# Expert stage of a two-layer decoder trunk: from 128-slot blocks per expert with weights cut in two to 32-slot units packed into five blocks with weights in plain float32

## The chip, the cores and the metric

The kernel runs on one core of a Trainium2 chip. The metric is device time in microseconds of one execution. Times are medians over the runs shown; everything read from a profile belongs to one profiled execution, whose span is given with it.

## The reference

256 tokens of width 1024 pass through two layers. Each layer has a mixer part (an S5 scan, retention and stick-breaking attention side by side), a norm, a feed-forward part and a second norm. Layer 0 has a dense SwiGLU; layer 1, the subject here, has a router with 8 experts of hidden width 688, of which each token takes the best two.

```python
def moe_swiglu(x, w_router, e_gate, e_up, e_down):
    xt = x.reshape(-1, d)                               # 256 x 1024
    logits = (xt @ w_router).astype(F32)                # 256 x 8
    top_val, top_idx = lax.top_k(logits, TOP_K)         # TOP_K = 2
    top_w = jax.nn.softmax(top_val, axis=-1)
    gates = jnp.sum(jax.nn.one_hot(top_idx, N_EXPERTS) * top_w[..., None], axis=1)
    out = jnp.zeros(xt.shape, F32)
    for e in range(N_EXPERTS):
        out = out + gates[:, e:e + 1] * swiglu(xt, e_gate[e], e_up[e], e_down[e])
    return out

def swiglu(x, w_gate, w_up, w_down):                    # 1024x688, 1024x688, 688x1024
    return (jax.nn.silu(x @ w_gate) * (x @ w_up)) @ w_down
```

Everything is float32. Of the 512 pairs of token and expert, the reference's routing of these inputs gives the eight experts 50, 75, 58, 31, 91, 61, 47 and 99.

## The kernel before

**Layout of the work.** Tokens stand in two tiles of 128 (t = 0, 1). All large products of the kernel are made of float32 numbers cut into two float32r parts: `mm3` makes three passes, high by high, high by low and low by high, into one PSUM bank. [...]

**The weight stream.** `Stream` holds one list of weight pieces in the order of use. A piece is up to 128 x 1032 numbers (516 KB). SyncE issues its DMA into a tile `st` (`load`, L361), ScalarE copies it as float32r to `wh` (L376), and VectorE, or GpSimd for some pieces, subtracts that from `st` to make `wl` (L380). Six `st` tiles, five pairs `wh`/`wl`, and four further `st2` tiles in the expert stage bound how far the stream runs ahead. The stream goes through both layers without a break, so the first pieces of the experts are loaded and cut while the mixers of layer 1 still run. `done` of a piece issues the load of a later one.

**The expert stage before.** `route` makes the logits of a token tile and the 0/1 choice `sel`; `places` ranks the tokens of each expert by a triangular matmul, and `one_hots` (L1202) makes from the ranks, per expert, a 128 x 128 matrix `Pf` (token by slot). Each expert has 128 slots. `gather(pr)` multiplies the tokens' two parts by the `Pf` of two experts: `xe_h`, `xe_l` hold 2 x 128 slots by 1024 (L1275, L1277). `gu` makes gate and up of one expert and one half of its hidden columns: 8 k tiles, each `mm3` of 128 slots by 344 columns. `prep` transposes and cuts the hidden values, `down` makes 6 k tiles by 1024 columns, and `y_h`, `y_l` (L1371, L1372) are the weighted results in two parts, which `scatter` sends back to the tokens with the transposed one-hots `PT`. A second pass over all weights follows if some expert has more than 128 tokens; here none has. The tail is the last norm and the DMAs of the output (L1474).

**What sets the order.** Each engine runs its instructions in one fixed order, worked out when the program is built, mostly that of the code. PSUM has eight banks (`Bank()`), given out in turn. Tiles of a pool with `bufs=n` rotate, and a new pool's tiles may lie where a closed pool's tiles lay; their first writer then waits for the last readers of those. The pool `mix` holds what the mixers need and is closed before the expert stage, whose pool `moe` takes its place.

Of the kernel before, what the change touches and what calls it, by code (L numbers as in the profile page):

```python
# [26 lines left out]
DFE = 688  # L27
DFP = 704
HFE = 344
NE = 8  # L30
TWO_PI = 2.0 * math.pi
# [8 lines left out]
for _n, _w in (("ident", 128), ("ntri", 128), ("nones", 128), ("blk64", 128), ("blk16", 128),  # L40
               ("rank", 128), ("iota", 128), ("i32", 32), ("sel", 8),
               ("iota8", 8)):
    CST[_n] = (_o, _o + _w)
    _o += _w
NCST = _o


def host_constants():
# [12 lines left out]
    put("iota", np.broadcast_to(p[None, :], (128, 128)))  # L61
    put("i32", (p[:, None] % 32 == np.arange(32)[None, :]))
    put("sel", (p[:, None] % 32 == np.arange(8)[None, :]))
    put("iota8", np.broadcast_to(np.arange(8)[None, :], (128, 8)))
    half = 32
# [25 lines left out]
KSPLIT = {256: (4, 4), 2 * FL: (2, 2, 2, 2), HFE: (3, 3, 2)}  # L91
KFIRST = (2, 2, 4)
HALVES = ((0, 512), (512, D))
CUTS = ((0, 512), (512, 768), (768, D))


def tiles_of(w, c0, n, split=None):
    """the column block [c0, c0 + n) of w [1024, .] as consecutive [128, kt * n] pieces"""
    out, k0 = [], 0
    for kt in split or KSPLIT[n]:  # L100
        out.append(w[k0 * 128:(k0 + kt) * 128, c0:c0 + n].reshape(kt, 128, n).transpose(1, 0, 2).reshape(-1))
        k0 += kt
    return out


def layout(inp):
    """the operands in the order in which the kernel reads them; nothing but moves and zero padding"""
# [32 lines left out]
    for n in ("moe_w_gate", "moe_w_up"):  # L140
        w[n] = np.concatenate([p for x in a[n] for y in x for hf in range(2) for p in tiles_of(y, hf * HFE, HFE)])
# [4 lines left out]
    w["moe_w_down"] = np.pad(a["moe_w_down"].reshape(-1, D), ((0, DFP - DFE), (0, 0)))  # L146
# [8 lines left out]
class Lanes:  # L155
# [15 lines left out]
    def urgent(self, gen, all_steps):  # L171
        """the first step, or all steps, issued ahead of what was emitted before them"""
# [26 lines left out]
PM = 2  # L199
# [5 lines left out]
URG2 = 60  # L205
# [7 lines left out]
def trunk(ctx, tc, I, out, dbg=None, layers=2):  # L213
# [5 lines left out]
    wst = ctx.enter_context(tc.tile_pool(name="wst", bufs=NST))  # L219
    whl = ctx.enter_context(tc.tile_pool(name="whl", bufs=NHL))  # L220
    act = ctx.enter_context(tc.tile_pool(name="act", bufs=1))
    psum = ctx.enter_context(tc.tile_pool(name="psum", bufs=8, space=PSUM))

# [3 lines left out]
    # functions that live in different tables keep their order of emission, so that tables change seldom  # L227
# [3 lines left out]
    def behind(x, y):  # L231
        """x after y in the order of their engine"""
# [18 lines left out]
    class Bank:  # L251
# [21 lines left out]
    def mm_narrow(b, o, h, wh, wl):  # L273
        """h: 64 rows of high parts over their low parts; wh: the high parts of 64 weight rows, twice"""
# [15 lines left out]
    # ---------------------------------------------------------------- weight stream  # L290
# [3 lines left out]
    def add_cols(key, name, n, specs=specs, split=None):  # L294
        """next column block of the array `name`"""
# [12 lines left out]
    def plan_moe(specs):  # L308
        def gu(e, hf):
            for part, name in (("g", "moe_w_gate"), ("up", "moe_w_up")):  # L310
                pos_in[name] = (2 * e + hf) * D * HFE
                add_cols((part, e, hf), name, HFE, specs)

        def dn(e):
            for k in range(6):
                add_rows(("dn", e, k), I["moe_w_down"], e * DFE + k * 128, min(128, DFP - k * 128), specs)

        for e in range(0, NE, 2):
            gu(e, 0)
            gu(e, 1)  # L320
            gu(e + 1, 0)
            dn(e)
            gu(e + 1, 1)
            dn(e + 1)

    for l in range(layers):
# [12 lines left out]
        else:  # L339
            plan_moe(specs)  # L340

    class Stream:
        def __init__(self, specs):
            self.specs = specs
            self.ld = self.sp = self.used = 0
            self.extra, self.ahead = None, NST
            self.act_after = self.dve_after = None
# [3 lines left out]
        def load(self):  # L351
# [4 lines left out]
            if self.extra is not None and i % 10 >= 6:  # L356
                st = self.extra.tile([128, CW], F32, name="st2", bufs=4)
            else:
                st = wst.tile([128, CW], F32, name="st")
# [5 lines left out]
        def split(self):  # L365
# [10 lines left out]
            x = S.activation(hv, st, AF.Copy)  # L376
            if self.act_after is not None:
                behind(x, self.act_after)
            on_pool = (self.extra is not None and i % 5 == PM) or i in self.pool_lo
# [3 lines left out]
            elif self.dve_after is not None:  # L383
                behind(x, self.dve_after)
# [17 lines left out]
        def done(self, key):  # L402
# [4 lines left out]
            while self.sp < self.used + NHL and self.sp < len(self.specs):  # L407
# [3 lines left out]
               + [((1, "u"), 0)] + [(("g", 0, 0), k) for k in range(2)])  # L411
# [17 lines left out]
    def ln_stats(sm, away=False, part=None):  # L429
        """mean (12), rstd (15), -mean * rstd (16)"""  # L430
# [12 lines left out]
    def ln_apply(t, r, y, sm, w_bc, b_bc, h, away=False):  # L443
        c = slice(h * 512, (h + 1) * 512)
        if away:
            # on the engines beside the vector engine
            W.act_after = S.activation(y[:, c], r, AF.Identity, scale=sm[:, 15:16], bias=sm[:, 16:17])
# [22 lines left out]
    # ---------------------------------------------------------------- S5 operands of a layer  # L470
    def s5_pre(l, mp, q, E):
        """what depends on the layer's parameters alone; q: the queue that loads them, E: the engine of the larger products"""
# [59 lines left out]
        # e^{4 i theta}  # L532
# [12 lines left out]
        def after(x):  # L545
            """behind the weights' splits that the engine has to make by now"""
# [6 lines left out]
        # rotation tables cos, sin of 4 theta c and the decay r^4 (0 where a pair's row begins)  # L553
# [20 lines left out]
        # input operands a^{3-i} Bbar, block-diagonal over the two groups of a pair  # L574
# [12 lines left out]
        # output operands C a^{j+1}: re, -im  # L587
# [21 lines left out]
        # within-chunk operator  # L609
# [43 lines left out]
    def rms_rstd(pool, b, cols, sq, blk, tag, bufs=2):  # L653
        """mean of squares over channel blocks by a block matrix; returns rstd tile [128, n]"""
# [7 lines left out]
    # ---------------------------------------------------------------- one layer's mixers  # L662
# [155 lines left out]
    late = []  # L818
    LNL = {}

    def layer(l, mp):
# [135 lines left out]
            # output projection: rows of the finished parts first  # L957
# [21 lines left out]
            for t in range(2):  # L979
# [16 lines left out]
            if l % 2:  # L996
                late.extend((l, "o", k) for k in order[5:])
                L.drain()
            for k in order[4:5] if l % 2 else order[4:]:
                W.done((l, "o", k))  # L1000
            W.act_after = None
            W.dve_after = RT.get("hot")
# [5 lines left out]
    # ---------------------------------------------------------------- dense SwiGLU  # L1008
    def ffn(l, fp):
# [20 lines left out]
            # the last, narrow block first and with the tokens stationary: it starts on the first token tile alone  # L1030
# [69 lines left out]
    # ---------------------------------------------------------------- top-2 of 8 experts  # L1100
# [412 lines left out]
```

## Time and profile before

| | us |
|---|---|
| median of 3 runs (743.38 to 743.99) | 743.42 |
| span of the profiled execution | 744.1 |
| PE busy in the span | 693.4 (93%) |
| VectorE, ScalarE, GpSimd busy | 552.8, 454.9, 266.4 |
| bytes read from HBM | 146.42 MB |

PE is TensorE's matmuls, PEld its weight loads, DVE VectorE, ACT ScalarE, POOL GpSimd and SP SyncE, whose busy time is not counted; a "q" behind an engine's name is its sequencer. The busy share over the whole span mixes the mixers of two layers, a dense feed-forward part, the router at about 475 to 500 us and the expert stage from there to the end. The change touches the program from the router on, so the windows from 490 us to the end are what is to be read.

### The profile page before, as it was taken

How to read it: one execution, taken by the hardware profiler on the slowest of the kernel's cores; microseconds unless marked ns; L12 is line 12 of the kernel's file. 1: busy time of each engine (PE TensorE's matmuls, PEld its weight loads, DVE VectorE, ACT ScalarE, POOL GpSimd, SP SyncE). 2: the span in 40 equal slices, each digit the busy share in tenths (PEclk: the TensorE clock that was granted, in tenths of full speed). 3: DMA queues.
4: the chain of work that ended last, by engine and by line, in shares of the span. 5: the costliest groups of instructions: out<-in, count | busy, mean ns of one | idle time of the engine just before them, and what ended most of it. 6: DMA issues, size and time to landing. Idle time of an engine off the chain costs nothing. (4 is left out here: it accounts for less than half of the span.)

```text
span 744.1 us, 12592 instructions
## 1 busy us (share of the span) xinstructions
PE 693.4 (93%) x4812; PEld 621.4 (84%) x4812; DVE 552.8 (74%) x756; ACT 454.9 (61%) x665; POOL 266.4 (36%) x245
## 2 busy tenths in 40 slices
PE   6989899989999999999899999968999999999993
PEld 6988777778999999988798887758889889899882
DVE  5998957588655455558867476599999986889976
ACT  5646686455444444453447985347878884888862
POOL 1734611599970000005014220354534322323441
PEclk9979999989999999999999999969999999999997
DMA  8844453356566666662473262338989987988911
GB/s 326 294 148 168 117 182 100 106 165 223 165 198 190 184 192 186 186 194 88 146 220 116 85 200 77 103 122 285 362 283 331 343 285 269 297 301 296 346 34 61
DMA packets 43987, 148.36 MB, mean 199 GB/s; under 512 B 5328, under 2 KB 5456, under 8 KB 43920
## 3 DMA queue, kind: packets, MB, share of 16 engines
q1 hardware_dynamic: 43776, 147.23, 60.5%
q8 instruction: 39, 0.64, 0.4%
q14 instruction: 28, 0.23, 0.1%
q10 hardware_dynamic: 144, 0.26, 0.1%
HBM read 146.42 MB, written 1.05 MB: 198 GB/s over the span
## 5 line engine op out<-in xcount | busy, mean ns | idle before, releaser
L380 DVE TENSOR_TENSOR wl<-st,wh 128x1024 fp32r<-128x1024 f32 (+4 forms) x235 | 308.8, 1335 | 111.8 <-ACT wh L376 111.2
L376 ACT ACTIVATE wh<-st 128x1024 fp32r<-128x1024 f32 (+5 forms) x275 | 275.4, 1020 | 159.7 <-PE bank L257 135.8
L380 POOL TENSOR_TENSOR wl<-st,wh 128x1024 fp32r<-128x1024 f32 (+4 forms) x40 | 100.6, 2521 | 274.5 <-ACT wh L376 274.4
L257 PE MATMUL bank<-xth,wh 128*128 128x256 f32 x608 | 175.1, 288 | 0.0
L257 PE MATMUL bank<-xtl,wh 128*128 128x256 f32 x608 | 172.5, 284 | 0.0
L257 PE MATMUL bank<-xth,wl 128*128 128x256 f32 x608 | 172.3, 283 | 0.0
L257 PEld LDWEIGHTS bank<-xth,wh 128*128 128x128 f32 x608 | 116.2, 191 | 2.0 <-issue 0.9
L257 PEld LDWEIGHTS bank<-xth,wl 128*128 128x128 f32 x608 | 116.1, 191 | 0.8 <-issue 0.5
L257 PEld LDWEIGHTS bank<-xtl,wh 128*128 128x128 f32 x608 | 116.0, 191 | 0.8 <-issue 0.2
L257 PE MATMUL bank<-wl,xe_h 128*128 128x344 f32 x256 | 82.1, 321 | 2.5 <-DVE wl L380 2.5
L257 PE MATMUL bank<-wh,xe_h 128*128 128x344 f32 x256 | 83.3, 325 | 0.0
L257 PE MATMUL bank<-wh,xe_l 128*128 128x344 f32 x256 | 81.9, 320 | 0.7 <-DVE xe_l L1277 0.7
L257 PEld LDWEIGHTS bank<-wl,xe_h 128*128 128x128 f32 x256 | 48.3, 189 | 3.1 <-DVE wl L380 3.1
L257 PEld LDWEIGHTS bank<-wh,xe_h 128*128 128x128 f32 x256 | 48.4, 189 | 1.8 <-ACT wh L376 1.0
L257 PEld LDWEIGHTS bank<-wh,xe_l 128*128 128x128 f32 x256 | 48.1, 188 | 1.0 <-DVE xe_l L1277 0.9
L257 PE MATMUL bank<-wl,hT_h 128*128 128x512 f32 (+3 forms) x102 | 40.5, 397 | 0.0
L257 PE MATMUL bank<-wh,hT_h 128*128 128x512 f32 (+1 forms) x102 | 39.8, 390 | 0.0
L257 PE MATMUL bank<-wh,xth 128*128 128x256 f32 (+1 forms) x112 | 31.3, 320 | 7.5 <-ACT wh L376 6.4
L257 PE MATMUL bank<-wh,f_h 128*128 128x512 f32 x88 | 35.3, 401 | 0.1
L257 PE MATMUL bank<-wl,f_h 128*128 128x512 f32 (+1 forms) x88 | 35.0, 397 | 0.0
L257 PE MATMUL bank<-wh,f_l 128*128 128x512 f32 x84 | 33.2, 397 | 1.7 <-DVE f_l L419 1.7
L257 PE MATMUL bank<-wh,hT_l 128*128 128x512 f32 (+1 forms) x85 | 32.6, 383 | 0.0
(301 smaller groups left out, 1234.9 us busy)
## 6 DMA issues: line engine op xcount, KB each, us to landing
st<-in_w_in_dram SPq DMA_DIRECT2D x47, 512.0 KB, 4.1
st<-in_moe_w_down_dram SPq DMA_DIRECT2D x40, 512.0 KB, 5.6
st<-in_moe_w_gate_dram SPq DMA_DIRECT2D x32, 516.0 KB, 5.5
st<-in_moe_w_up_dram SPq DMA_DIRECT2D x32, 516.0 KB, 5.2
st<-in_ffn_w_down_dram SPq DMA_DIRECT2D x21, 512.0 KB, 4.3
st<-in_ffn_w_gate_dram SPq DMA_DIRECT2D x20, 512.0 KB, 4.3
st<-in_ffn_w_up_dram SPq DMA_DIRECT2D x20, 512.0 KB, 4.3
st<-in_w_out_dram SPq DMA_DIRECT2D x16, 512.0 KB, 3.9
```

The costliest lines, as they stand in the source:

```text
L257: PE.matmul(o, lhsT, rhs, start=part not in self.begun, stop=True, skip_group_check=True)
L376: x = S.activation(hv, st, AF.Copy)
L380: x = (G if on_pool else V).tensor_tensor(lv, st, hv.bitcast(F32), op=OP.subtract)
```

## The change

Tokens of an expert sit in **units** of 32 slots. Four units make a block of 128 slots, and there are five blocks, 20 units. Fifteen units belong to fixed experts (two to each of experts 0 to 6, one to expert 7: units 1 to 3 of block j belong to expert (3j + u - 1) // 2). The first unit of each block is free: an expert with more than 64 tokens (32 for expert 7) takes free units in turn, and which expert a free unit belongs to is computed on the chip by `places`, written to `unit` and loaded into a TensorE register for each block. If more than five free units are needed, the whole stage runs again on the tokens left over, and a third time above ten. By the counts above the experts need 0, 1, 0, 0, 1, 0, 0 and 3 free units.

A product of one k tile and one block is now four matmuls in plain float32 with 32 slots each, whose results go to partitions 0, 32, 64 and 96 of one bank; the first reads its weights at an address from the register. The loops are turned: k tile by k tile, and in it the five blocks with all experts. For this the weights lie in memory k tile by k tile for all eight experts: a **chunk** `ch` is 128 rows by 8 x 344 numbers, 1.409 MB, loaded by two DMAs of 704 KB, and a ring of 7 chunks runs ahead. There are 32 chunks for gate and up (2 hidden halves x 2 matrices x 8 k tiles) and 18 for down (3 cuts of the output columns x 6 k tiles of 128, 128 or 96 rows), 68.16 MB. No expert weight is cut in two any more. The stream of the earlier stages ends with layer 1's `w_out`, and its pools are closed ahead of the expert stage.

The main parts of the diff (what `Stream` no longer needs, `host_constants`, the removed `gu`, `prep`, `down` and `scatter`, and the second pass are left out):

```diff
+        w[n] = np.ascontiguousarray(a[n][0].reshape(NE, KT, 128, 2, HFE).transpose(3, 1, 2, 0, 4)).reshape(-1)
...
-                            normed(0, *zs[0], lnw[:, 0], lnw[:, 1])
-                            places(0)
-                            RT["hot"] = places(1)
-                            normed(1, *zs[1], lnw[:, 0], lnw[:, 1])
+                            places()
+                            for t_ in range(2):
+                                normed(t_, *zs[t_], lnw[:, 0], lnw[:, 1])
...
+    def places():
+        pb = Bank()
+        pb.mm(pb.t[:, 0:8], rank_b[:, 0], sel[:, 0])
...
+        V.tensor_tensor(over, pb.t[:, 16:24], C["cap"], op=OP.subtract)
+        V.tensor_copy(pos, pb.t[:, 0:16].rearrange("p (t e) -> p t e", t=2))
...
+        V.tensor_scalar(ui[:, 0:16], eu, float(NE - 1), None, op0=OP.min)
...
+    def one_hots(p, pool):
+        for t in range(2):
+            sl = RT["slots"][:, :, 0:wb]
+            V.tensor_scalar(tmp, sl, nm[:, t, 0:1], None, op0=OP.is_equal)
+            V.scalar_tensor_tensor(P[:, t], sl, nm[:, t, 1:2], tmp, op0=OP.is_equal, op1=OP.add)
...
+    class Chunks:
...
+            t = self.pool.tile([128, NE * HFE], F32, name="ch", bufs=NCH)
+            v = t[:rows, 0:NE * cols]
+            for h in range(2):
+                n = NE * cols // 2
+                SP.dma_start(v[:, h * n:(h + 1) * n], bass.AP(tensor=ap.tensor, offset=ap.offset + o + h * n, ap=[[NE * cols, rows], [1, n]]))
...
     def moe(l):
         with tc.tile_pool(name="moe", bufs=1) as mp:
-            W.extra, W.ahead = mp, 10
-            while W.ld < min(W.sp + W.ahead, len(W.specs)):
-                W.load()
+            with tc.high_priority(offset=URG):
+                RT["P"] = one_hots(0, mp)
+            first_chunks = Chunks(mp)
...
+                unit = [nc.values_load(RT["unit"][0:1, p * NDYN + j:p * NDYN + j + 1], engines=[mybir.EngineType.PE], min_val=0, max_val=NE - 1)
+                        for j in range(NB)]
...
+                    for k, o in ((0, Pg[:, t]), (1, Pw)):
+                        G.tensor_scalar(o, RT["slots"][:, :, 0:wb], nm[:, t, k:k + 1], gates[:, t, k:k + 1], op0=OP.is_equal, op1=OP.mult)
...
+                def units(b, o, lhs, j, ch, cols):
+                    b.mm(o[0:32], lhs[:, j * wb:j * wb + 32], ch[:, bass.ds(unit[j], 1), :].rearrange("p a n -> p (a n)"), part=0)
+                    if not p:
+                        for u in range(1, 4):
+                            b.mm(o[32 * u:32 * u + 32], lhs[:, j * wb + 32 * u:j * wb + 32 * u + 32], ch[:, (3 * j + u - 1) // 2, :], part=u)
+
+                def project(name, hf, between=()):
+                    acc = [Bank() for _ in range(NB)]
+                    for kt in range(KT):
+                        if kt in between:
+                            between[kt]()
+                        ch = WM.get(name, hf, kt)
+                        for j in range(NB):
+                            units(acc[j], acc[j].t[:, 0:HFE], xe[:, kt], j, ch, HFE)
+                        WM.done(name, hf, kt)
+                    return acc
...
+                def hidden(hf):
+                    gt = project("moe_w_gate", hf, {} if hf else {0: lambda: gather(range(4)), 4: lambda: gather(range(4, 8))})
+                    for j in range(NB):
+                        fn(ms[:wb, j], gt[j].t[:wb, 0:HFE], AF.Silu)
+                    up = project("moe_w_up", hf, {4: weigh} if not hf else {})
+                    for j in range(NB):
+                        V.tensor_tensor(hs[:wb, j, 0:HFE], ms[:wb, j], up[j].t[:wb, 0:HFE], op=OP.mult)
+                        for k in range(3):
+                            b.tr(b.t[:, k * wb:(k + 1) * wb], hs[:wb, j, k * 128:(k + 1) * 128], ident[:wb, :wb])
...
+                for c, (c0, c1) in enumerate(DCUTS):
+                    for k in range(6):
+                        ch = WM.get("down", c, k)
+                        for j in range(NB):
+                            units(acc[j], acc[j].t[:, 0:w], hT[:rows, k // 3, k % 3], j, ch, w)
+                        WM.done("down", c, k)
...
+            total = nc.values_load(RT["unit"][0:1, 16:17], min_val=0, max_val=16)
+            with tc.If(total > NDYN):
+                experts(1, Chunks(mp))
```

Two places show how instructions move. The first is SyncE's queue at the end of the weights of layer 1's `w_out` (`st` is a tile of the old stream, `ch` half a chunk of the new one). Before:

```order
L361 DMA st<-in_w_out_dram 128x1024 [waits DMAHW6_49,DVE_49]
L361 DMA st<-in_moe_w_gate_dram 128x1032 [waits DVE_49]
L361 DMA st<-in_moe_w_gate_dram 128x1032 [waits DMAHW0_49,DVE_49,Activation_49]
L361 DMA st<-in_moe_w_gate_dram 128x688 [waits DMAHW1_49,DVE_49]
L361 DMA st<-in_moe_w_up_dram 128x1032 [waits DMAHW4_49,DMAHW2_49,DVE_49]
```

And with the change:

```order
L361 DMA st<-in_w_out_dram 128x1024 [waits DVE_49]
L1274 DMA ch<-in_moe_w_gate_dram 128x1376 [waits DMAHW3_49,DMAHW2_49,DMAHW4_49,DMAHW0_49,DMAHW5_49,DVE_49,DMAHW6_49,PE_49,DMAHW7_49,Activation_49,Pool_49]
L1274 DMA ch<-in_moe_w_gate_dram 128x1376 [waits DMAHW1_49]
L1274 DMA ch<-in_moe_w_gate_dram 128x1376 x6
...
L1292 DMA lnw<-in_ln_ffn_w_dram 128x1024 [waits DMAHW6_49]
L1293 DMA lnw<-in_ln_ffn_b_dram 128x1024 [waits DMAHW7_49]
L1274 DMA ch<-in_moe_w_gate_dram 128x1376 [waits DMAHW0_49,PE_49]
```

The first expert weights waited only for a piece to be cut; now the first chunk waits for all engines, the next thirteen halves for nothing but queues, and from the fifteenth on for a chunk that TensorE has read.

The second place is TensorE at the end of the gather (`Pf` or `P` is the one-hot matrix, `xe` the gathered tokens, `wh`/`wl` parts of a cut weight). Before:

```order
L257 MATMUL bank<-Pf_5177,xl 128x256 x5
L257 MATMUL bank<-wh,xe_h 128x344 [waits DMAHW3_49,DMAHW4_49,DMAHW2_49,DMAHW5_49,DMAHW1_49,DMAHW6_49,DMAHW0_49,DMAHW7_49,Activation_49,Pool_49]
L257 MATMUL bank<-wl,xe_h 128x344
L257 MATMUL bank<-wh,xe_h 128x344 [waits Activation_49]
L257 MATMUL bank<-wl,xe_h 128x344 [waits DVE_49]
```

And with the change:

```order
L281 MATMUL bank<-P_5202,xl 128x128
L281 ISA
L281 MATMUL bank<-ch,xe 32x344 [waits DMAHW1_49,DMAHW0_49,Activation_49]
L281 MATMUL bank<-ch,xe 32x344 x3
L281 ISA
L281 MATMUL bank<-ch,xe 32x344 x4
L281 ISA
```

Three full matmuls per k tile and expert have become four of 32 partitions per k tile and block, each four behind a register operation (`ISA`) that forms the address of the free unit's weights.

## Rows read from the trace of the kernel before

**Rows 1.** Windows by stage: us; busy PE, PEld, DVE, ACT, POOL (count); PEclk; DMA share; GB/s.

```profile
490.00:512.00 22.00, 17.85 (x99) 16.86 (x100) 20.10 (x51) 13.41 (x21) 11.21 (x7) 0.73 0.64 214
512.00:700.00 188.00, 185.93 (x1081) 168.15 (x1080) 167.49 (x176) 148.69 (x191) 66.41 (x34) 1.00 0.91 311
...
712.00:731.00 19.00, 18.87 (x105) 15.68 (x103) 13.20 (x20) 8.21 (x13) 7.35 (x4) 1.00 0.00 0
731.00:744.10 13.10, 0.92 (x6) 0.71 (x6) 6.99 (x12) 2.85 (x7) 3.15 (x2) 0.62 0.24 87
```

**Rows 2.** The chain around the first expert work: start us, duration us, engine, line, operation.

```profile
489.48 1.27 POOL L448 TENSOR_TENSOR xtok<-xtok,lnw 128x512 f32<-128x512 f32 x1 [3.56 <-ACT xtok L447]
...
489.69 1.08 DVE L1160 SCALAR_TENSOR_TENSOR rtw<-rtw,ln_s,rneg 128x8 f32<-128x8 f32 x1
...
492.41 2.25 DVE L1163 CAST rtw<-ix 128x2 f32<-128x2 uint32 x1
...
495.44 0.22 DVE L1165 SCALAR_TENSOR_TENSOR sel<-cst,rtw 128x8 bf16<-128x8 f32 x1
...
501.28 0.49 PE L257 MATMUL bank<-wh,xe_h 128*128 128x344 f32 x1
```

**Rows 3.** SyncE's queue in the 50 us before the expert stage, same columns.

```profile
445.28 7.05 SPq L361 DMA_DIRECT2D st<-in_moe_w_gate_dram  x3
```

**Rows 4.** Windows with the DMA engines filled, columns as in the first group.

```profile
520.00:540.00 20.00, 20.00 (x110) 17.60 (x109) 19.70 (x19) 16.94 (x22) 11.32 (x5) 1.00 1.01 361
580.00:600.00 20.00, 20.00 (x111) 17.60 (x110) 16.35 (x17) 15.34 (x20) 7.94 (x3) 1.00 1.00 363
...
584.00:592.00 8.00, 8.00 (x35) 5.93 (x35) 7.78 (x6) 6.51 (x8) 2.75 (x2) 1.00 1.02 405
```

**Rows 5.** DMA queue of the weights, 488 to 712: packets, MB, share of 16 engines.

```profile
q1 hardware_dynamic: 19504, 65.87, 85.8%
```

**Rows 6.** Groups of instructions from 490 to 712: busy us, mean ns, idle before.

```profile
L257 PE MATMUL bank<-wh,xe_h 128*128 128x344 f32 x254 | 82.7, 325 | 0.0
...
L380 DVE TENSOR_TENSOR wl<-st,wh 128x1032 fp32r<-128x1032 f32 x50 | 70.0, 1429 | 6.2 <-ACT wh L376 6.2
...
L1331 DVE TENSOR_TENSOR hs<-m_s,bank 128x344 f32<-128x344 f32 x15 | 7.6, 506 | 4.9 <-PE bank L257 4.7
...
L249 ACT ACTIVATE m_s<-bank 128x344 f32<-128x344 f32 x16 | 7.1, 444 | 0.7 <-PE bank L257 0.7
```

**Rows 7.** TensorE in the router, float32 with 32 output columns: start us, duration us.

```profile
474.93 0.43 PE L257 MATMUL bank<-xt,rw 128*32 128x128 f32 x8
475.28 0.50 PE L257 MATMUL bank<-wh,mtl 128*128 128x512 f32 x1
```

**Rows 8.** The 32-wide router matmuls by themselves: duration ns min/median/max.

```profile
L257 PE MATMUL bank<-xt,rw x32: 272/285/297, 474.9 to 488.1; 128*32 128x128 f32 x32
```

**Rows 9.** TensorE in the scan's operands of layer 0, full-width matmuls: same columns.

```profile
101.23 0.28 PE L257 MATMUL bank<-xth,wl 128*128 128x256 f32 x1
101.35 1.89 PE L257 MATMUL bank<-s5g,prm 128*128 128x256 f32 x8
```

**Rows 10.** TensorE in the same scan, 64-wide float32 matmuls: same columns.

```profile
87.13 0.98 PE L257 MATMUL bank<-s5e,vmat 128*64 128x63 f32 x26
```

**Rows 11.** Register operations at the branch: duration ns min/median/max.

```profile
L1480 SPq FUSED_REGOPS  x1: 191/191/191, 706.6 to 706.6; - x1
...
L1480 PEldq TENSOR_LOAD <-cmi x1: 487/487/487, 731.4 to 731.4; - x1
```

**Rows 12.** A window with TensorE two thirds busy, columns as in the first group.

```profile
350.00:356.00 6.00, 4.00 (x38) 3.76 (x36) 6.00 (x4) 0.00 (x0) 5.16 (x2) 1.00 0.55 184
```

**Rows 13.** The last scatter, columns as in the second group.

```profile
730.37 0.47 ACT L1371 ACTIVATE y_h<-bank,gs 128x256 fp32r<-128x256 f32 x1 [2.50 <-PE bank L257]
730.88 0.48 DVE L1372 SCALAR_TENSOR_TENSOR y_l<-bank,gs,y_h 128x256 fp32r<-128x256 f32 x1 [0.40 <-ACT y_h L1371]
...
731.47 0.45 PE L257 MATMUL bank<-y_l,PT 128*128 128x256 f32 x2
```

More of the change, by code (lines that the diff above doesn't have):

```diff
@@ L26 @@
 DFF = 2752
-DFE = 688
-DFP = 704
 HFE = 344
 NE = 8
+NB = 5
+NDYN = 5
+NSTAT = 3 * NB
+NCH = 7
+KM = (128, 128, 96)
+DCUTS = ((0, 344), (344, 688), (688, D))
 TWO_PI = 2.0 * math.pi
@@ L45, with slot_names @@
 NCST = _o
+FREE = 1000.0
+def slot_names():
+    n = np.zeros((NB, 128), np.float32)
+    n[:, :32] = FREE + 32 * np.arange(NB)[:, None] + np.arange(32)
+    n[:, 32:] = np.arange(NB * 96).reshape(NB, 96)
+    return np.ascontiguousarray(np.broadcast_to(n.reshape(1, -1), (128, NB * 128)))
 def host_constants():
@@ L64, in host_constants @@
     put("iota8", np.broadcast_to(np.arange(8)[None, :], (128, 8)))
+    put("iota16", np.broadcast_to(np.arange(16)[None, :], (128, 16)))
+    own = np.array([32 * min(2, NSTAT - 2 * e) for e in range(NE)], np.float32)
+    put("one8", 1.0)
+    put("cap", own[None, :])
+    put("e64", 64.0 * np.arange(NE)[None, :])
+    put("dynb", (FREE - own - 64.0 * np.arange(NE))[None, :])
+    put("j32", 32.0 * np.arange(8)[None, :])
     half = 32
@@ L198 @@
 NST = 6
-PM = 2
 PEO = 'sk'
@@ L355, in load @@
             _, ap, rows, kt, n = self.specs[i]
[L356 to L359, printed above, removed]
+            st = wst.tile([128, CW], F32, name="st")
             v = st[:rows, :kt * n]
@@ L375, in split @@
             hv, lv = h[:rows, :kt * n], l[:rows, :kt * n]
[L376 to L379, printed above, removed]
+            S.activation(hv, st, AF.Copy)
+            on_pool = i in self.pool_lo
             x = (G if on_pool else V).tensor_tensor(lv, st, hv.bitcast(F32), op=OP.subtract)
@@ L410, in trunk @@
     POOL_LO = ([((0, "gu"), k) for k in range(4)] + [((0, "g", 0), 0)] + [((1, n), k) for n in ("sv", "rv0") for k in range(2)]
-               + [((1, "u"), 0)] + [(("g", 0, 0), k) for k in range(2)])
+               + [((1, "u"), 0)])
     W = Stream(specs)
@@ L996, in layer @@
             if l % 2:
-                late.extend((l, "o", k) for k in order[5:])
                 L.drain()
-            for k in order[4:5] if l % 2 else order[4:]:
+            for k in order[4:]:
                 W.done((l, "o", k))
-            W.act_after = None
-            W.dve_after = RT.get("hot")
             dump(f"x1_{l}0", x_tok[0])
@@ L1198, in one_hots @@
-    def one_hots(Pf, t, pr, after=None):
-        pos, self_f = RT["pos"], RT["sel"]
-        for i in range(2):
-            e = 2 * pr + i
-            x = V.tensor_scalar(Pf[:, t, i], C["iota"], pos[:, t, e:e + 1], self_f[:, t, e:e + 1], op0=OP.is_equal, op1=OP.mult)
-            if after is not None:
-                behind(x, after)
-        return x
-    def gate_values(x):
-        rank_b, sel, gb = RT["rank"], RT["selb"], RT["gb"]
+            S.activation(xh[:, t, c], x_tok[t][:, c], AF.Copy)
@@ new lines, in one_hots @@
+    def one_hots(p, pool):
+        wb = 32 if p else 128
+        nm = RT["nm"]
+        P = pool.tile([128, 2, NB, wb], F32R, name=f"P{wb}")
+        tmp = pool.tile([128, NB, wb], F32, name=f"Pt{wb}")
+        if p:
+            later = pool.tile([128, 2, 2], F32, name="later")
+            V.tensor_scalar(later, nm, -32.0 * NDYN * p, None, op0=OP.add)
+            nm = later
+        for t in range(2):
+            sl = RT["slots"][:, :, 0:wb]
+            V.tensor_scalar(tmp, sl, nm[:, t, 0:1], None, op0=OP.is_equal)
+            V.scalar_tensor_tensor(P[:, t], sl, nm[:, t, 1:2], tmp, op0=OP.is_equal, op1=OP.add)
+        return P, nm
@@ new lines, in gate_values, with __init__, add, load @@
+            V.tensor_tensor(g[:, t, 1:2], e2[:, 1:2], g[:, t, 0:1], op=OP.mult)
+        return g
+    class Chunks:
+        def __init__(self, pool):
+            self.pool, self.keys, self.ld, self.used, self.t = pool, [], 0, 0, {}
+            at = {}
+            for hf in range(2):
+                for name in ("moe_w_gate", "moe_w_up"):
+                    for kt in range(KT):
+                        self.add(at, (name, hf, kt), name, 128, HFE)
+            for c, (c0, c1) in enumerate(DCUTS):
+                for hf in range(2):
+                    for k in range(3):
+                        self.add(at, ("down", c, 3 * hf + k), "moe_w_down", KM[k], c1 - c0)
+            for _ in range(NCH):
+                self.load()
+        def add(self, at, key, name, rows, cols):
+            if (name, key[1]) == ("moe_w_gate", 1) and key[2] == 0:
+                assert at[name] == KT * 128 * NE * HFE
+            self.keys.append((key, name, at.get(name, 0), rows, cols))
+            at[name] = at.get(name, 0) + rows * NE * cols
+        def load(self):
+            if self.ld >= len(self.keys):
+                return
+            key, name, o, rows, cols = self.keys[self.ld]
+            self.ld += 1
+            t = self.pool.tile([128, NE * HFE], F32, name="ch", bufs=NCH)
+            v = t[:rows, 0:NE * cols]
+            ap = I[name]
+            for h in range(2):
+                n = NE * cols // 2
+                SP.dma_start(v[:, h * n:(h + 1) * n], bass.AP(tensor=ap.tensor, offset=ap.offset + o + h * n, ap=[[NE * cols, rows], [1, n]]))
+            self.t[key] = v.rearrange("p (e n) -> p e n", e=NE)
+        def get(self, *key):
+            return self.t[key]
+        def done(self, *key):
+            assert self.keys[self.used][0] == key
+            self.t.pop(key)
+            self.used += 1
+            self.load()
@@ L1495, in trunk @@
                 raise NotImplementedError
+    streams.close()
     if layers == 2:
```

432 lines of the change are left out of this document (135 added, 297 removed).

## The prediction

> **What bounds the kernel now.** I read the table of 40 slices first, for where the load changes, then windows by stage, the groups of the expert stage, the DMA queue, and the timelines at the stage's two ends. From 512 to 700 PE is busy for 185.93 of 188 us at a granted clock of 1.00, with the DMA engines at 0.91 [rows 1]. Its commonest matmul, 128 x 344, has no idle time in front of it [rows 6]. The window from 712 to 731 settles it: no weight moves any more and PE is still busy for 18.87 of 19 us. So TensorE, with three passes per product, sets the expert stage. The cutting of the weights (VectorE 1.43 us for a piece of 1032 columns [rows 6]) hides behind it: that it goes is worth nothing by itself. The transfers are a close second limit: 65.87 MB at 0.858 of the engines in 224 us [rows 5].
>
> **Until the first expert product.** PE's own program is the same up to the ranks in the router, so I leave the first 490 us as they are (bounds: 2 us either way, because the other engines lose some cuts there). The first chunk's DMA waits for the last readers of the closed pools. In before's terms these are VectorE's 489.69 + 1.08 and GpSimd's 489.48 + 1.27 [rows 2], so 490.8. [...] The places are made on VectorE: the choice of the second token tile comes at 495.44 before, but behind a tiny cast that took 2.25 us beside GpSimd's cut [rows 2], which is gone, so some 493.5. Then come about 18 small instructions at 0.25 (near that choice's 0.22), 4.5 us, and four comparisons of 640 columns. At 506 ns for 344 columns [rows 6] these are 0.94 each, 3.8 us, or twice that if GpSimd's six instructions of the same width stretch them as it stretched the cast. The matrix P is ready between 502 and 506. TensorE's five register loads stand ahead of the gather; at 487 ns and a register operation of 191 each [rows 11] they are 3.4 us, and lie beside the comparisons.
>
> The first half of the gather has 16 matmuls of 512 and 16 of 128 columns, 10,240 columns. A 256-column float32r matmul has the next one 0.12 us behind it [rows 9], so 4.8 us, and 9.6 at the lower clock level, to which PE has fallen here (mean 0.73 between 490 and 512 [rows 1]). I put the first expert product at 512 (508 to 515); before it came at 501.28 [rows 2]. This start costs 11 us.
>
> **The products on PE.** One block and k tile is a group of four matmuls with 32 output partitions, two passes each over 344 columns. There are 32 chunks of gate and up and 18 of down with five blocks each: 250 groups. For the pass I use two rows. Eight full-width float32 passes of 256 columns take 1.89 us [rows 9]; the last outlasts its slot by 0.16, as the single matmul ahead of it does (0.28, successor after 0.12), so a slot is 1.73 / 8 = 0.216 us, 0.84 ns a column, 0.29 us for 344. In the router four 32-wide tiles with two passes each, eight records, take 0.43 us [rows 7], while one alone lasts 0.285 [rows 8]. All eight thus start within 0.145 us; one behind another they would need 8 x 0.107. The four tiles run side by side. A group therefore costs between 2 x 0.29 = 0.58 us and, if the whole 0.145 us for 128 columns scales with length, 2 x 0.145 x 344 / 128 = 0.78. I take 0.60, near the full-width row, since most of the 0.145 can be start-up: 150 us, with 145 and 195 as ends.
>
> Other work in PE's order: the second half of the gather 4.8 us (full clock); ten transposes and ten one-column float32 products for the gates, about 4 (two passes of 0.107 each, and the one-column ones little less than half); the change from gate to up, where five of eight banks wait for Silu at 444 ns [rows 6], 0.75 twice; the two ends of a hidden half, where five multiplications at 506 ns [rows 6] precede their transposes, 3 twice; two scatters between cuts of down, each 20 matmuls of 344 columns at 0.16 and 0.6 of waiting for the first result, 3.8 twice. Sum 24. PE alone would end at 512 + 150 + 24 = 686. From 512 to 731.9 before there were 220 us of work here; now 174.
>
> **The transfers.** 68.16 MB of chunks and 1.05 MB of norm weights are 69.2 MB. Filled windows of 20 us moved 361 and 363 GB/s, one of 8 us 405 [rows 4]; the queue's bytes over its fully busy time are 65.87 / (0.858 x 224) = 343 [rows 5]. I take 362: 191 us, last landing at 683.6 (405: 663; 343: 694). Nothing holds a load back except the ring: by 512 five of seven chunks are there, and a chunk then takes 3.9 us to arrive against 3.0 on PE. So PE waits a little in the long runs of groups, and the ring fills again during the gather, the hidden ends and the scatters. The last chunk adds 3 us on PE: 686.6. Both limits give the same time; where they alternate some 2 us more are lost: last group at 689. Waiting a fifth of the time should not cost the clock: with PE busy for 4.00 of 6 us it stayed at 1.00 [rows 12].
>
> **The end.** After the last group come the two weighted copies of its block (0.47 and 0.48 at 256 columns [rows 13], some 0.55 each at 344, with 0.25 of latency), ten scatter matmuls 1.6, and the addition 0.6 that before was made by PE for these columns: 3.5. From the end of the last scatter (731.47 + 0.45 [rows 13]) to the span's end are 12.2 us before, with the same norm, output DMAs and branch. With 0.4 for copies of the blocks ahead that are still in the queue that is 16.1: 705.1. The profiled span, 744.1, lies 0.7 above the median shown, 743.42; so 704.4, and I say 704.
>
> [...] The rows above have four tiles at work together, with an end at 0.78. [...]
>
> **Rivals.**
> *Packed tiles hinder each other.* The four tiles stream four different rows of weights; the router's 0.145 us for 128 columns allows 0.78 us a group [rows 7, 8], the full-width row 0.58. [...] For it: the 0.145 itself. Against: start-up explains it as well. [...]
> *Transfers stay at the old stage's rate.* 311 GB/s [rows 1] gives 715 + 3 + 16 = 733; 295, its mean with both ends, 742, no change. Against: loads then stood waiting for cuts, and here for nothing.
> *The register address holds the array up (slower).* Each group begins with a register operation and a matmul whose address comes from it. 191 ns for the operation on SyncE [rows 11] and eight passes dispatched at 0.98 / 26 = 0.038 us each [rows 10] make 0.49, hidden below 0.58 if PE's sequencer runs ahead of the array. If it does not and each group is drained first, operation and fill come on top: 0.58 + 0.19 + 0.2 = 0.97 us, 242 us in all, 794. It decides from 0.77 us a group, where the time passes 743. For it: 250 such places, all on the engine that bounds, and none in before. Against: the separate queue of PE's sequencer in the trace.
> *The stage runs twice.* With more than five free units all weights are read again, 190 us more, about 890. The reference's routing asks for exactly five; a token whose choice flips on rounding could make it six. The count nearest to its limit, 61 of 64, is three tokens off.
>
> **Chances.** Forecast 0.60 (own range 694 to 716: 343 or 405 GB/s, groups of 0.58 to 0.65, first product at 508 to 515); packed tiles 0.17, of which 0.02 beyond 743; old transfer rate 0.04, half of it no change; register address 0.17; twice 0.02. What a measurement can tell from no change is 0.2%, 1.5 us. Faster: 0.60 + 0.14 + 0.02 = 0.76; same: 0.02 + 0.01 from packed tiles = 0.03; the rest, 0.21, slower. The range of 8 in 10 takes the forecast, most of the packed tiles and the slow transfers: 690 to 744.
>
> **What would show it.** Right: between 520 and 680 the DMA share near 1.0 at some 360 GB/s, PE at 75 to 90% with clock 1.00, its idle time ended by DMA; the four matmuls of a group together and the next group 0.6 us later; first product at 512, last near 689; no splitting of weights on ScalarE and VectorE. Wrong: PE full while the DMA share sinks to 0.8 or less (groups too slow; then gaps ahead of the first of four point to the register, longer passes to the packing); a first product after 516; a load that waits in the ring all the time; or two passes through the chunks.

## The result and the profile after

The changed kernel's median is 716.5 us over four runs (709.0 to 723.3), against 743.6 for the kernel before; the ratio, 0.960 with a 95% interval of 0.955 to 0.965, leaves out the longest run, which counts as slow. The forecast was 704, with 690 to 744 as the range: faster as forecast, with 39 us expected and 27 found. The median lies just outside the forecast's own range of 694 to 716. The profiled execution was that longest run, 723.28 us with a span of 721.6, some 7 us above the median; where its length matters, this is said.

Windows by stage of the changed kernel, columns as in [rows 1] (us; busy time of PE, PEld, DVE, ACT, POOL; granted clock; DMA share; GB/s):

```profile
490.00:512.00 22.00, 10.15 (x53) 7.70 (x55) 13.82 (x47) 4.55 (x10) 14.82 (x8) 0.57 0.72 287
512.00:612.00 100.00, 100.00 (x1301) 49.34 (x1297) 5.37 (x10) 12.07 (x24) 2.06 (x3) 1.00 1.02 414
612.00:706.00 94.00, 75.90 (x840) 38.00 (x828) 13.87 (x26) 9.59 (x19) 0.00 (x0) 0.89 0.87 232
706.00:721.60 15.60, 3.28 (x24) 3.01 (x20) 9.47 (x16) 2.42 (x7) 2.85 (x2) 0.75 0.20 71
```

From 512 to 612, gate and up, PE is busy throughout at a granted clock of 1.00, and the queue moves 414 GB/s. From 612 on, down, PE is busy for 75.90 of 94 us and its granted clock falls to 0.89 in the mean. Until the loads end, near 694, the DMA engines are about as busy as before, yet they move much less. The rate in 40 slices of 604 to 692 us shows how:

```profile
DMA  9999999999999999999999999999999999999997
GB/s 413 410 423 408 400 223 215 195 244 263 410 315 223 205 228 243 353 395 223 228 178 230 260 358 343 215 211 218 223 357 347 242 232 208 232 376 369 242 218 196
```

The share stays at nine tenths or more, while the rate falls from 410 to some 220 and recovers to 350 or 400 every six slices, 14 us. That is the time of three down chunks, of 128, 128 and 96 rows. Waits of the down stretch (engine, line, what it waited for: us in total, times, longest):

```profile
PE bank L281 <- DMA ch<-in_moe_w_down_dram: 17.9, 10, 4.5
```

The start of the stage, which answers to [rows 2] (start us, us, engine, line, operation):

```profile
493.04 0.86 DVE L1150 SCALAR_TENSOR_TENSOR rtw<-rtw,ln_s,rneg 128x8 f32<-128x8 f32 x1
...
495.24 12.94 SPq L1274 DMA_DIRECT2D ch<-in_moe_w_gate_dram  x14
...
496.82 0.22 DVE L1155 SCALAR_TENSOR_TENSOR sel<-cst,rtw,ohs 128x8 bf16<-128x8 f32 x1
...
500.37 1.38 DVE L1227 SCALAR_TENSOR_TENSOR P<-slots,slotname,Pt 128x640 fp32r<-128x640 f32 x1
...
502.38 0.88 DVE L1227 SCALAR_TENSOR_TENSOR P<-slots,slotname,Pt 128x640 fp32r<-128x640 f32 x1
...
503.75 0.76 PE L281 MATMUL bank<-P,xh 128*128 128x512 f32 x1 [6.43 <-DVE P L1227]
...
511.76 0.50 PE L281 MATMUL bank<-ch,xe 128*32 x4
```

The first chunk is issued at 495.24, the choice stands at 496.82 + 0.22, the second P is ready at 503.26, the gather runs from 503.75 and the first product comes at 511.76. The group of the gate and up products at fixed addresses (busy us, mean ns | idle), and the register operations (duration ns min/median/max), which answer to [rows 6, 11]:

```profile
L281 PE MATMUL bank<-ch,xe 128*32 128x344 f32 x960 | 93.3, 453 | 0.0
```

```profile
L281 PEldq FUSED_REGOPS  x250: 46/46/51, 509.5 to 703.6; - x125
```

No cut of an expert weight is left on ACT or DVE.

### The profile page after: what moved, and what is told of

It reads as the page before. It is cut to its first block, busy times and chain, and to the rows that moved or that the text cites. A ratio compares the mean times of both kernels' runs of the same rounds, so it can differ in the third digit from the quotient of the medians.

```text
span 721.6 us, 13775 instructions
## 1 busy us (share of the span) xinstructions
PE 649.9 (90%) x5655; PEld 511.2 (71%) x5655; DVE 372.4 (52%) x582; ACT 295.3 (41%) x476; POOL 188.8 (26%) x207
## 4 chain that ended last, share of the span: by engine, by line
PE 47%; DMA 16%; issue 12%; DVE 11%; ACT 8%; POOL 4%; SPq 0%; DVEq 0%; POOLq 0%; ACTq 0%
PE bank L281 46%; DMA ch<-in_moe_w_down_dram 11%; DMA ch<-in_moe_w_up_dram 4%; DVE wl L378 3%; ACT wh L376 2%; ACT r_sw L935 2%; PE bank L290 2%; DMA st<-in_w_in_dram 1%; POOL wl L378 1%; ACT L273 1%; ACT s5y L705 1%; POOL s5w L495 1%; DVE xtok L437 1%; DVE f_l L415 1%; DVE s5s L683 1%
## 5 line engine op out<-in xcount | busy, mean ns | idle before, releaser
L378 DVE TENSOR_TENSOR wl<-st,wh 128x1024 fp32r<-128x1024 f32 (+1 forms) x121 | 155.8, 1289 | 99.5 <-ACT wh L376 99.3
L376 ACT ACTIVATE wh<-st 128x1024 fp32r<-128x1024 f32 (+3 forms) x131 | 136.3, 1046 | 126.4 <-PE bank L281 105.5
L281 PE MATMUL bank<-ch,xe 128*32 128x344 f32 (+1 forms) x1280 | 94.1, 453 | 0.0
L281 PE MATMUL bank<-ch,hT 128*32 (+1 forms) x720 | 63.3, 505 | 18.1 <-DMA ch<-in_moe_w_down_dram 17.9
L281 PEld LDWEIGHTS bank<-ch,xe 128*32 128x32 f32 x1280 | 41.5, 110 | 50.0 <-issue 49.0
L281 PEld LDWEIGHTS bank<-ch,hT 128*32 128x32 f32 (+1 forms) x720 | 28.4, 121 | 51.7 <-issue 41.3
L378 POOL TENSOR_TENSOR wl<-st,wh 128x1024 fp32r<-128x1024 f32 (+1 forms) x10 | 22.7, 2300 | 132.6 <-ACT wh L376 132.6
L1400 DVE SCALAR_TENSOR_TENSOR y<-bank,gs,y 128x344 fp32r<-128x344 f32 (+1 forms) x15 | 8.6, 573 | 75.1 <-ACT y L1399 75.1
L1399 ACT ACTIVATE y<-bank,gs 128x344 fp32r<-128x344 f32 (+1 forms) x15 | 8.2, 545 | 79.6 <-PE bank L281 79.2
L281 PE MATMUL bank<-wh,xtl 128*128 128x256 f32 (+1 forms) x112 | 30.5, 314 | 0.0
## 6 DMA issues: line engine op xcount, KB each, us to landing
ch<-in_moe_w_gate_dram SPq DMA_DIRECT2D x32, 688.0 KB, 11.0
ch<-in_moe_w_up_dram SPq DMA_DIRECT2D x32, 688.0 KB, 11.5
ch<-in_moe_w_down_dram SPq DMA_DIRECT2D x16, 688.0 KB, 19.3
```

What stands on the lines that cost most here:

```text
L281: PE.matmul(o, lhsT, rhs, start=part not in self.begun, stop=True, skip_group_check=True)
L378: x = (G if on_pool else V).tensor_tensor(lv, st, hv.bitcast(F32), op=OP.subtract)
L1399: S.activation(y[:wb, 0, j, 0:w], a, AF.Copy, scale=gs[:wb, j:j + 1])
L1400: V.scalar_tensor_tensor(y[:wb, 1, j, 0:w], a, gs[:wb, j:j + 1], y[:wb, 0, j, 0:w].bitcast(F32), op0=OP.mult, op1=OP.subtract)
```

## The experiments

**A. Is it the number of rows?** Two theories of the slow stretch fitted the trace: transfers that fill fewer than 128 partitions are slow, or the down array (or the down phase) is. The first kernel pads the 96-row chunks to 128 rows with zeros; it moves 2.1 MB more and changes nothing else.

```diff
-KM = (128, 128, 96)
+KM = (128, 128, 128)
```

> The 96-row down chunks are padded with zero rows to 128 (2.2 MB more, no more TensorE columns). Theory A, a transfer that fills fewer than 128 partitions is slow: the down chunks move at the 414 GB/s of the gate and up chunks, all 71.3 MB are there by about 668 us, TensorE bounds the stage, the last group ends near 678 and the median is 693 to 697, with a spread between runs of under 2 us. Rival B, the down array itself or the down phase reads slowly: 25.2 MB at the same 266 GB/s, 95 us from 608, and the median is 720 to 730.

Measured: 692.0 us median (688.7 to 694.2), ratio to the kernel before 0.929 (0.926 to 0.932). Windows, and the rate in 40 slices of 604 to 672:

```profile
512.00:612.00 100.00, 100.00 (x1301) 49.42 (x1297) 5.26 (x10) 12.07 (x24) 1.97 (x3) 1.00 1.02 414
612.00:677.00 65.00, 65.00 (x836) 32.95 (x829) 14.07 (x27) 9.77 (x20) 0.00 (x0) 1.00 0.91 367
```

```profile
GB/s 398 418 414 414 418 405 421 418 416 411 405 421 414 414 414 401 418 414 414 411 414 414 418 421 411 417 423 395 414 414 421 418 395 417 417 427 408 354 190 117
```

414 GB/s through gate, up and down, no stretch in which PE waits, clock 1.00. With more to move the stage is 29 us shorter from 612 on (65 against 94, the latter in the changed kernel's longest run); by the medians it is 24 us. Rival B is out. The time lies 1 us below the expected 693 to 697, and the runs spread over 5.5 us instead of under 2, which the last section comes back to.

The second kernel moves exactly the bytes of the changed one, in chunks of 128, 112 and 112 rows.

```diff
-KM = (128, 128, 96)
+KM = (128, 112, 112)
...
-b.tr(b.t[:, k * wb:(k + 1) * wb], hs[:wb, j, k * 128:(k + 1) * 128], ident[:wb, :wb])
+b.tr(b.t[:, k * wb:(k + 1) * wb], hs[:wb, j, sum(KM[:k]):sum(KM[:k]) + 128], ident[:wb, :wb])
```

> The same bytes as the changed kernel, but the three k tiles of a hidden half have 128, 112 and 112 rows instead of 128, 128 and 96. Theory A in its strict form (any transfer under 128 partitions is slow): two of three chunks are slow, the rate in the down phase falls below 266 GB/s, median 725 to 745. Theory A in a weaker form (slow in proportion to the partitions missing, 96 worse than 112): rate 350 or more, median 695 to 703. Rival B: as the changed kernel, 709 to 718.

Measured: 730.4 us (726.8 to 732.8), ratio 0.981 (0.978 to 0.985). A window of its down stretch:

```profile
612.00:706.00 94.00, 70.96 (x763) 34.94 (x755) 12.45 (x23) 7.49 (x15) 0.00 (x0) 0.91 1.01 231
```

231 GB/s at a share of 1.01: the strict form. This is near the 220 that the changed kernel moves while a 96-row chunk is among those under way, and with two short chunks of three the rate stays low (230 over 640 to 680); it costs 14 us more than one of three. What a chunk of 112 or 96 rows moves by itself was not measured.

**B. One transfer, or what is being filled together?** Each chunk is loaded by rows instead of by columns: two DMAs of 64 partitions (48 for the short chunks), together the same partitions and bytes.

```diff
-                n = NE * cols // 2
-                SP.dma_start(v[:, h * n:(h + 1) * n], bass.AP(..., ap=[[NE * cols, rows], [1, n]]))
+                n = rows // 2
+                SP.dma_start(v[h * n:(h + 1) * n, :], bass.AP(..., ap=[[NE * cols, n], [1, NE * cols]]))
```

> The two DMAs of each chunk, gate and up too, take 64 (or 48) partitions with all 8 x 344 columns each, instead of all partitions with half the columns. Theory A as a matter of the single transfer: gate and up fall to the 130 to 270 GB/s of the slow stretches too, 45 MB take 170 us or more, median over 760. Theory A as a matter of which partitions are being filled at one moment: the two halves complement each other, gate and up stay near 414 GB/s, median 705 to 725. Rival B: no change against the changed kernel in gate and up, 709 to 718.

Measured: 824 us (815.0 and 833.0). Gate and up, where the changed kernel has 414 GB/s:

```profile
512.00:612.00 100.00, 67.41 (x696) 33.18 (x692) 4.81 (x9) 8.60 (x18) 0.27 (x1) 0.91 1.01 225
```

225 GB/s with the engines full, about half. So it is a matter of the single transfer, and not of the down array. That the two halves complement each other and are issued one behind the other does not help.

**C. The number of partitions, or where they lie?** On padded chunks, one DMA fills the even and the other the odd partitions: 64 partitions each again, with the same rows of 11008 bytes.

```diff
+                n = rows // 2
+                SP.dma_start(v[h::2, :], bass.AP(..., offset=ap.offset + o + h * NE * cols, ap=[[2 * NE * cols, n], [1, NE * cols]]))
```

> As half_rows (64 partitions a DMA, rows of 11008 bytes), but on padded chunks and with one DMA filling the even partitions and the other the odd ones. [...] Theory D, what counts is the number of partitions of one transfer: 220 GB/s as in half_rows, median 815 or more.

Measured: 688.6 us (688.0 and 689.2).

```profile
512.00:612.00 100.00, 100.00 (x1301) 60.31 (x1290) 7.06 (x14) 12.19 (x25) 0.26 (x1) 1.00 1.01 420
```

420 GB/s. The same count of partitions, 64 a transfer, gives 420 GB/s when it is spread over all 128 and 225 when it is one neighbouring half: the place decides, not the count. The time is just under the 690 to 697 expected if the place decides; this execution came to the stage some 5 us earlier than pad128's. Spreading the partitions also spreads the rows of memory that one transfer reads. That was not tried alone, but the 112-row chunks read memory in the pattern of the 128-row ones and are slow all the same (in rows112 the whole mixture moves 231). Why the place decides no run shows, and neighbouring against spread was compared only for 64 partitions. For 96, in the slices above the rate falls to about 220 while a 96-row chunk is among those in flight. How a transfer's rows are shared out among the engines was not tried, so what makes 96 and 112 as slow as this stays open.

**D. Does the register address cost anything?** On the padded kernel the free unit reads expert 7's weights at a fixed address.

```diff
-b.mm(o[0:32], lhs[:, j * wb:j * wb + 32], ch[:, bass.ds(unit[j], 1), :].rearrange("p a n -> p (a n)"), part=0)
+b.mm(o[0:32], lhs[:, j * wb:j * wb + 32], ch[:, 7, :], part=0)
```

> As pad128, but the first unit of each block reads the weights of expert 7 at a fixed address instead of the address from the register (so the output of the free units is of the wrong expert). If the register address costs TensorE nothing, as the 0.29 us between passes says, the time is pad128's within 1 us. If it costs its 46 ns per group, 250 groups give 11 us: 683 to 686.

Measured: 691.4 us (689.1 and 693.7) against 692.0. First and last start of the products of both kernels, pad128 first (duration ns min/median/max, first and last start):

```profile
L281 PE MATMUL bank<-ch,xe x1280: 452/452/477, 511.7 to 615.8; 128*32 128x344 f32 x137, 128*32 x46
...
L281 PE MATMUL bank<-ch,hT x720: 446/452/477, 618.0 to 676.4; 128*32 x180
```

```profile
L281 PE MATMUL bank<-ch,xe x1280: 452/452/477, 506.6 to 610.7; 128*32 128x344 f32 x183
...
L281 PE MATMUL bank<-ch,hT x720: 446/452/477, 612.9 to 671.3; 128*32 128x344 f32 x120, 128*32 128x336 f32 x60
```

From first to last start it is 676.4 - 511.7 = 164.7 us with the register and 671.3 - 506.6 = 164.7 without. The 250 register operations of 46 ns, which the second kernel does not have, cost nothing. That the one profile lies 5 us earlier than the other arose long before the stage (last section).

**E. The clock at the gather.** PE waits for the places for 6.4 us and then gathers at a granted clock of 0.67 in the mean: 0.50 from 503.75 to 508.5, 0.93 from there to 511.7. Fourteen spare matmuls of 512 columns fill the wait.

```diff
+                if not p:
+                    wu = Bank()
+                    for _ in range(14):
+                        behind(wu.mm(wu.t[:, 0:512], xh[:, 0, 0:128], xh[:, 0, 0:512]), RT["ranked"])
                 unit = [nc.values_load(RT["unit"][0:1, p * NDYN + j:p * NDYN + j + 1], ...
```

> As pad128, with 14 spare matmuls of 512 columns in the 6.5 us in which TensorE waits for the places, ahead of the gather (nothing reads their result). If the gather is slow because of the clock that fell while TensorE waited, its 16 wide matmuls come 0.22 instead of 0.43 us apart, the time from its start to the first product falls from 8.0 to about 5 us, and the median by 3 us, to 689. If the gather waits for something else (its copies, the register loads), the first product stays 8 us behind the start and the median at 692.

Measured: 688.8 us (688.1 to 690.9), ratio 0.924 (0.920 to 0.928). The start of the gather, before (changed kernel) and with the spare matmuls:

```profile
504.74 0.63 PE L281 MATMUL bank<-P,xh 128*128 128x512 f32 x1
505.17 0.63 PE L281 MATMUL bank<-P,xl 128*128 128x512 f32 x1
```

```profile
499.38 0.47 PE L281 MATMUL bank<-P,xh 128*128 128x512 f32 x1 [1.30 <-DVE P L1228]
499.69 0.40 PE L281 MATMUL bank<-P,xl 128*128 128x512 f32 x1
499.93 0.40 PE L281 MATMUL bank<-P,xh 128*128 128x512 f32 x1
...
504.94 1.36 PE L281 MATMUL bank<-ch,xe 128*32 x16
```

Wide matmuls come 0.23 us apart instead of 0.43, and from the gather's start to the first product it is 5.56 us instead of 8.01 (pad128's gather, from 503.66 to 511.7, takes as long). It is the clock, as expected: in pad_warm's windows from 499 to 505 it is granted at 1.00. But the stretch after it grew. The down stretch shows where:

```profile
611.85 11.82 PE L281 MATMUL bank<-ch,hT 128*32 x160
623.95 3.19 PE L281 MATMUL bank<-ch,hT 128*32 x40 [0.28 <-DMA ch<-in_moe_w_down_dram]
627.34 3.10 PE L281 MATMUL bank<-ch,hT 128*32 x40 [0.20 <-DMA ch<-in_moe_w_down_dram]
630.37 3.44 PE L281 MATMUL bank<-y,PT 128*128 128x344 f32 x20
```

PE, earlier by then, meets chunks that have not landed: short waits here, all for DMA, which pad128 does not have (there 240 products of one cut run in one piece of 17.56 us). This cut, with two waits, takes 630.37 - 611.85 = 18.52 us from its first product to the scatter, against 17.48 in pad128. From first to last start it is 671.7 - 504.9 = 166.8 us instead of 164.7. The 2.4 us gained were given back to the transfers, almost whole: from the gather's start to the last product's start the profiled executions take 172.3 us, and 172.7 in pad128. So the median of 689 was met mostly by luck. The gather starts at 499.38 here and at 503.66 there, for the reason of the last section.

**F. Both.** The spare matmuls with the even and odd partitions.

> pad_warm with the even and odd partitions of even_odd. In pad_warm TensorE gained 2.5 us in the gather and gave about 2 back in short waits for down chunks. If the transfers at 414 GB/s were what took it back, the 420 GB/s of even_odd (71.3 MB in 170 us instead of 172) return nearly all of it: first product to last group 165 us, median 686 to 687.5. If something else did (the order of banks, the copies), first product to last group stays 167 us and the median 688 to 689.

Measured: 687.4 us (687.0 to 688.7), ratio 0.924 (0.922 to 0.926): the lowest median, though the intervals do not separate it from pad_warm and even_odd. The waits for down chunks are gone: each cut of down runs in one piece again.

```profile
612.66 17.56 PE L281 MATMUL bank<-ch,hT 128*32 x240
...
633.49 17.56 PE L281 MATMUL bank<-ch,hT 128*32 x240
...
654.33 17.16 PE L281 MATMUL bank<-ch,hT 128*32 x240
```

The time is within the expectation, which by the last section says little, and first to last start did not come back to 165 (671.0 - 504.6 = 166.4). In this execution the clock dipped for two windows, with PE busy throughout:

```profile
538.00:542.00 4.00, 4.00 (x36) 2.84 (x38) 0.16 (x1) 1.59 (x5) 0.00 (x0) 0.84 1.03 425
542.00:546.00 4.00, 4.00 (x44) 1.64 (x40) 0.00 (x0) 0.00 (x0) 0.00 (x0) 0.74 0.99 416
```

That is 0.16 and 0.26 of 4 us, 1.7 us as an estimate. So the experiment shows that the waits went, and leaves open what a run without the dip would give.

## Why the prediction was right, and where it was not

*What bounded before, and that the cuts were worth nothing:* right, as far as it was tried. In pad128 PE is busy throughout from 512 to 677, and the sum of its work at the end of this section gives the time without a term for the cuts of 1.43 us [rows 6]. A kernel that loses only the cuts was not run.

*The start, 512:* met, by errors that cancel, so by luck. The first chunk was issued at 495.24, not 490.8. The same logits step that stands at 489.69 in [rows 2] stands at 493.04 here, 3.4 us later. The router's products, which answer to [rows 8]:

```profile
L281 PE MATMUL bank<-xt,rw x32: 272/297/422, 477.2 to 491.3; 128*32 128x128 f32 x32
```

So 2.3 of the 3.4 us stand ahead of the router (477.2 against 474.9): this execution was late from layer 0 on, where its clock between 184 and 190 was 0.56, against 0.72 in the one of before. The rest arose within the router, whose order the change alters. The last landing at 683.6 counts the 191 us of transfers from 492.5, 1.7 us behind an issue at 490.8; no run shows that term. Here the first bytes move at 496.2, 0.96 us behind the issue, and from 497.75 to 500 the rate is 423 GB/s. The places then took less: 18 small instructions 2.7 us instead of 4.5 (mostly 0.15 to 0.2 each), and the four comparisons 3.5; of the two longer ones one took 1.38 and the other 0.88, with GpSimd busy beside both. The gather, at a clock of 0.67, took 8.0, within what was reckoned.

*0.60 us a group:* right, at the lower end. The thirty groups of a down cut, and the scatter behind them, in pad128:

```profile
618.01 17.56 PE L281 MATMUL bank<-ch,hT 128*32 x240
635.49 3.41 PE L281 MATMUL bank<-y,PT 128*128 128x344 f32 x20
```

They take 635.49 - 618.01 = 17.48 us, 0.583 each; the full-width row [rows 9] gave 0.58. The rival in which packed tiles hinder each other falls: a pass of four tiles takes 0.29 us, like one full-width pass. Other work on PE: 165 - 250 x 0.583 = 19 us instead of 24.

*The register rival:* falls, by D. PE's own register operation took 46 ns against SyncE's 191 [rows 11], and it was hidden behind the products.

*The transfers, 362 GB/s:* this is the step that failed. "I take 362" was a mean over windows that already held both rates, 405 in one and, over longer ones, 361 and 363 [rows 4]. I took it for one speed with noise. It was two speeds: 414 while all transfers under way fill all partitions, and some 220 while shorter ones are among them. Before's last down piece of each expert has 64 rows, 256 KB; the first line below is their DMA issues (count, size, us to landing). A window with one of them under way shows the low rate there too:

```profile
st<-in_moe_w_down_dram SPq DMA_DIRECT2D x8, 256.0 KB, 6.7
```

```profile
592.00:596.00 4.00, 4.00 (x27) 4.00 (x27) 3.94 (x5) 3.28 (x5) 0.00 (x0) 1.00 1.01 257
```

This is read from the trace; the kernel before was not run with padded pieces. With two speeds the gate and up stage comes out faster than forecast and down slower. The mean itself was not far off: 69.2 MB between 495.24 and 694.68, where PE's last wait for a chunk ends, are 347 GB/s, within the bounds of 343 and 405. What the one speed hid is where the loads come late. The last wait ends at 694.68, where 683.6 was forecast for the last landing. Behind it PE has three chunks left instead of one, and they take 11.35 us, at first at a clock of 0.50 (694.68 to 698), instead of 3. So the last product came at 706 instead of 689, in a run some 7 us above the median. The result lies between the forecast and the rival in which the old rate stays (733), and the range, wide because of the rivals, held it. In that rival's sum 295 GB/s gives 745 by its own terms and not 742.

*The clock while waiting:* "should not cost the clock" was wrong. Where PE waits for down chunks it fell to 0.89 on average, and PE took 75.90 us of busy time for what takes 65.00 in pad128. Behind four of the ten waits the products are slow (40 take about 3.1 us elsewhere in this trace):

```profile
637.25 8.36 PE L281 MATMUL bank<-ch,hT 128*32 x80 [4.46 <-DMA ch<-in_moe_w_down_dram]
...
662.02 4.79 PE L281 MATMUL bank<-ch,hT 128*32 x40 [1.72 <-DMA ch<-in_moe_w_down_dram]
668.84 7.89 PE L281 MATMUL bank<-ch,hT 128*32 x80 [2.02 <-DMA ch<-in_moe_w_down_dram]
...
694.68 11.35 PE L281 MATMUL bank<-ch,hT 128*32 x120 [3.36 <-DMA ch<-in_moe_w_down_dram]
```

The idle time of the window in [rows 12] is nearly all one gap, of 2.00 us. The changed kernel has the same gap at the same place, and there the clock fell behind it. Gap and window, before first:

```profile
355.77 0.33 PE L266 MATMUL bank<-cst,xtok 128*128 128x128 f32 x1 [2.00 <-DVE xtok L441]
359.00:362.00 3.00, 2.64 (x21) 2.41 (x21) 1.92 (x4) 2.46 (x7) 0.00 (x0) 1.00 0.00 0
```

```profile
358.02 0.33 PE L290 MATMUL bank<-cst,xtok 128*128 128x128 f32 x1 [1.98 <-DVE xtok L437]
359.00:362.00 3.00, 3.00 (x16) 2.79 (x15) 2.87 (x7) 1.35 (x4) 0.00 (x0) 0.50 0.39 153
```

So a gap of 2 us left the clock alone in one execution and cost it in another, and one window was too little to forecast from. What decides it is not shown.

*The end, 16.1:* right. The last scatter begins with the last block's results:

```profile
705.96 3.33 PE L281 MATMUL bank<-y,PT 128*128 128x336 f32 x20
```

The last group ended just ahead, at 705.9 by this, and the span 15.7 later.

The sum that would have held, with 414 GB/s and the rest as predicted, is that of PE alone: 512 + 150 + 24 + 16 = 702; the padded kernel shows it with the smaller terms, 512 + 146 + 19 + 15.5 = 692, its span.

## What to carry to other kernels

When a rate is read from windows, ask whether it is one rate or a mean of two, and what the slow windows have in common: the shape of the transfer is the first thing to compare, and the DMA share does not show it (1.01 at 225 GB/s and at 420). Pad a transfer to 128 partitions, or spread its rows, even where that moves more bytes: here 2.1 MB more made the kernel 24 us faster. When a second limit lies close, a gain on the first is given back to it (in E almost all of 2.4 us), so the next edit goes to the other one.

## What the runs showed of the hardware that was not expected

Transfers to 64 neighbouring partitions moved 225 GB/s, those to 64 alternate partitions 420, both at a DMA share of 1.01. Four matmuls of 32 output partitions in float32 take as long as one of 128 (0.583 us against 0.58 reckoned from [rows 9]). And two executions differ by some 5 us before the expert stage: in layer 0 the granted clock falls in some executions and not in others, with PE busy in both. Windows of pad128 and of static_u0, whose programs are the same there:

```profile
184.00:190.00 6.00, 6.00 (x25) 5.23 (x25) 2.04 (x3) 1.06 (x1) 5.76 (x6) 0.55 0.54 173
```

```profile
184.00:190.00 6.00, 6.00 (x54) 6.00 (x53) 3.46 (x2) 2.13 (x3) 5.84 (x6) 1.00 0.50 163
```

Six busy us at 0.55 and at 1.00. Nothing in the program differs up to there; what decides it was not tried. Comparisons of kernels by a few us are better made from first to last product than by the whole time.
